# Attention values of the differential heads: one projection of 512 columns in place of two of 256, and a later turn

## Chip, cores and metric

The kernel runs on one core of a Trainium2 chip. The metric is device time in microseconds (us), from the start to the end of one execution.

## What is computed

A macaron layer in fp32 for one sequence of 512 tokens and 1024 features: half a SwiGLU feed-forward, a token mixer, another half feed-forward, each on a normalised input, and a last norm. The change lies in the mixer. Four differential heads (128 wide, two softmax maps each) and eight dilated heads (64 wide) share one input projection. Cut to what matters:

```python
proj = h @ w_in
qa, ka, va, qb, kb, vb = split(proj, each 512 wide)
# differential heads, H=4, two maps of 64 features, values of 128
s = q_blk @ k.T * scale + bias                  # causal, blocks of 128 queries
p = softmax(s);  a = p[:, :, 0] - lam * p[:, :, 1]
oa = rmsnorm(a @ va, subln_gain) * (1 - lam0)
# dilated heads, H=8: three windows, merged by their weights
ob = dilated_attention(qb, kb, vb, ...)
mixed = concat([oa, ob]) @ w_out
```

## The kernel before

Tokens are 4 blocks of 128, features 8 blocks of 128 (KD). Products run on TensorE in fp32r with both operands split into a high and a low part: one product of blocks becomes three (`mm3`: high by high, high by low, low by high). Weights come by DMA in units of 128 x 1024 (512 KB) into a `raw` buffer, of which there are three. ScalarE casts the high part (`high`, line 893), VectorE subtracts for the low part (`low`, line 897), each in two halves of 512 columns; there are three places for split units in `w_all`.

The attention is a schedule written by hand. `plan` lists the stages: q0 to q7 are query and key projections (q0 to q3 of one differential head each, q4 to q7 of two dilated heads each), v0 to v3 the values, 256 features a stage: v0 and v1 of the differential heads, v2 and v3 of the dilated ones. Each stage is 8 chunks of products, and one loop runs over the chunks: iteration t is called step t here. `put(t, rank, f)` hangs other work on a step: ranks below 10 are issued ahead of the step's chunk, others behind it, and within a step by rank. TensorE, VectorE and ScalarE keep the order of issue. At a step's end at most one queued low half and one queued cast are issued; a low half is issued at the earliest one step after its cast. `ahead(n)` at the first use of unit n queues the split of unit n+2 and starts the load of unit n+3.

A query stage takes one step per feature block: three products of 512 columns for queries (`pq`) and three for keys (`pk`). Seven steps after the start its banks are evacuated: `tq` and `tk` (VectorE), casts (ScalarE), rests (VectorE), DMAs to the other half of the partitions; head 0 has a form without DMAs (`evac_now`). A value stage (`v_chunks`) takes two steps for each of 4 token blocks: twelve products a step, with 128 tokens of x as the weights and 256 columns of weights moving, then ScalarE writes the result to a value tile.

`attention(u, s)` hangs a head's own work on the steps from s on: `score` (two products, one VectorE operation that adds the bias and finds the extreme, line 1061, and one exponential on ScalarE, line 1064), one a step; `combine` (lines 1068 to 1075), which merges the two maps of a block. Scores use two PSUM banks in turn. Then, for a differential head, `turn(m, i)`, which transposes the blocks 0..i of query block i by TensorE into a bank with tag `t` (two of them) and copies it by ScalarE, and `values(m, i)`, which multiplies by the values, two steps later. They start at step max(s + 5, end of the head's value stage), in four rounds two steps apart; nine steps after that begin `squares`, `mean`, `scale`, `finish`. In the order before, head 0's scores stand beside v0 and head 1's beside v1.

Product banks (`mm_bank`) have one tag with four buffers, shared by queries, keys, values and each head's output `po`. The tile with tag `tx` (128 x 3072, one buffer) serves the feed-forward and, in the attention, the turned blocks of the dilated heads.

## Time and profile before

| | |
|---|---|
| median of 3 runs | 930.6 us (930.59 to 932.77) |
| profiled execution | 930.6 us, span 928.8 us |
| TensorE (PE) busy | 921.3 us, 99% |
| VectorE (DVE) busy | 727.5 us, 78% |
| ScalarE (ACT) busy | 542.8 us, 58% |
| the attention's steps | about 346 to 545 us |
| value products (`pv`, 3 lines x 128) | 36.3, 36.2 and 36.2 us of records |

Records of products overlap, as a product is issued while the one before it drains; the interval between their starts is what they cost. "Idle before" and the releaser in brackets tell what an engine waited for.

### The profile page before, as it was taken

The page shows a single profiled execution, that of the slowest core. Times are in us where ns is not written, and L with a number is a line of the kernel's source. Part 1 is how long each engine was busy: PE and PEld are TensorE (multiplying, and loading weights), DVE is VectorE, ACT ScalarE, POOL GpSimd, SP SyncE. Part 2 cuts the span into 40 slices and gives each one's busy share as a digit, 9 for nine tenths or more (in the row PEclk, how much of TensorE's full clock was granted, in tenths as well). Part 3 has the DMA queues.
Part 4 walks back from the last instruction along what each step waited for, and adds up shares of the span by engine and source line. Part 5 has one row for each costly group of instructions (what it writes and reads, how often), then busy time and mean ns, then how long its engine had stood idle before and what let it go on. Part 6 is the DMA issues. An engine that isn't in the chain of part 4 may idle for free.

```text
span 928.8 us, 17112 instructions
## 1 busy us (share of the span) xinstructions
PE 921.3 (99%) x6402; PEld 853.8 (92%) x6402; DVE 727.5 (78%) x1501; ACT 542.8 (58%) x1122; POOL 98.3 (11%) x117
## 2 busy tenths in 40 slices
PE   9999999999999999999999999999999999999997
PEld 7889999999999999988979778889999999999997
DVE  7797887677888897668876556797888777888784
ACT  7455664355664575556766664455666455665573
POOL 0001101112202100000000003110111012110100
PEclk9999999999999999999999999999999999999999
DMA  7456646578757562434343113454774677875542
GB/s 259 127 147 149 160 126 178 134 183 223 189 134 201 141 177 92 136 96 129 96 136 92 68 49 132 115 172 103 180 193 118 163 200 191 201 192 149 140 128 91
DMA packets 59860, 136.71 MB, mean 147 GB/s; under 512 B 6832, under 2 KB 8112, under 8 KB 59776
## 3 DMA queue, kind: packets, MB, share of 16 engines
q1 hardware_dynamic: 45776, 110.14, 36.7%
q0 software_dynamic: 14000, 25.47, 17.6%
q8 instruction: 50, 0.82, 0.4%
q14 instruction: 34, 0.28, 0.1%
HBM read 130.30 MB, written 2.14 MB: 143 GB/s over the span
## 4 chain that ended last, share of the span: by engine, by line
PE 97%; DVE 2%; DMA 0%; issue 0%; DVEq 0%
PE pv L935 2%; PE pv L934 2%; PE pv L933 2%; PE pq L123 2%; PE pwo L123 2%; PE pq L124 2%; PE pq L125 2%; PE pk L125 2%; PE pk L123 2%; PE pk L124 2%; PE pwo L124 2%; PE pwo L125 2%; PE pua L123 2%; PE pua L124 2%; PE pua L125 2%; PE pda L124 1%
## 5 line engine op out<-in xcount | busy, mean ns | idle before, releaser
L1064 ACT ACTIVATE pr<-pr,mx 128x128 f32<-128x128 f32 (+3 forms) x64 | 36.0, 563 | 34.4 <-DVE mx L1061 34.1
L1061 DVE CUSTOM_DVE_ANT_0 pr<-sc,strip 128x128 f32<-128x128 f32 (+3 forms) x64 | 30.7, 487 | 22.4 <-PE sc L1059 22.0
L391 ACT CAST w<-s2b 128x512 fp32r<-128x512 f32 x50 | 31.0, 620 | 16.4 <-DVE s2b L373 14.9
L395 DVE TENSOR_TENSOR w<-s2b,w 128x512 fp32r<-128x512 f32 x50 | 34.2, 685 | 7.3 <-ACT w L391 7.3
L391 ACT CAST w<-s2a 128x512 fp32r<-128x512 f32 x46 | 28.6, 621 | 18.7 <-DVE s2a L373 15.8
L395 DVE TENSOR_TENSOR w<-s2a,w 128x512 fp32r<-128x512 f32 x46 | 31.5, 685 | 6.5 <-ACT w L391 6.5
L150 POOL TENSOR_TENSOR sq<-sq,sqt 128x512 f32<-128x512 f32 x7 | 10.9, 1563 | 240.2 <-ACT sqt L149 240.1
L933 PE MATMUL pv<-w,xh 128*128 128x256 f32 x128 | 36.3, 283 | 0.0
L935 PE MATMUL pv<-w,xh 128*128 128x256 f32 x128 | 36.2, 283 | 0.0
L934 PE MATMUL pv<-w,xl 128*128 128x256 f32 x128 | 36.2, 283 | 0.0
L123 PE MATMUL pq<-xh,w 128*128 128x512 f32 x64 | 26.3, 410 | 0.0
L123 PE MATMUL pwo<-mh,w 128*128 128x512 f32 x64 | 25.6, 399 | 0.0
L124 PE MATMUL pq<-xl,w 128*128 128x512 f32 x64 | 25.1, 393 | 0.0
L125 PE MATMUL pq<-xh,w 128*128 128x512 f32 x64 | 25.1, 392 | 0.0
L125 PE MATMUL pk<-xh,w 128*128 128x512 f32 x64 | 25.1, 392 | 0.0
L124 PE MATMUL pk<-xl,w 128*128 128x512 f32 x64 | 25.0, 391 | 0.0
L123 PE MATMUL pk<-xh,w 128*128 128x512 f32 x64 | 25.0, 391 | 0.0
L124 PE MATMUL pwo<-ml,w 128*128 128x512 f32 x64 | 25.0, 390 | 0.0
L125 PE MATMUL pwo<-mh,w 128*128 128x512 f32 x64 | 25.0, 390 | 0.0
L934 PEld LDWEIGHTS pv<-w,xl 128*128 128x128 f32 x128 | 24.5, 191 | 0.3
L933 PEld LDWEIGHTS pv<-w,xh 128*128 128x128 f32 x128 | 24.4, 191 | 0.2
L935 PEld LDWEIGHTS pv<-w,xh 128*128 128x128 f32 x128 | 24.5, 191 | 0.0
(709 smaller groups left out, 3996.9 us busy)
## 6 DMA issues: line engine op xcount, KB each, us to landing
raw_qk<-wqk_dram SPq DMA_DIRECT2D x16, 512.0 KB, 3.4
raw0bg<-wst_dram SPq DMA_DIRECT2D x9, 512.0 KB, 5.1
raw_gua<-wgu_dram SPq DMA_DIRECT2D x8, 512.0 KB, 3.6
raw0ag<-wst_dram SPq DMA_DIRECT2D x8, 512.0 KB, 4.8
raw0ad<-wdg_dram SPq DMA_DIRECT2D x8, 512.0 KB, 5.1
strip<-bias_rows SPq DMA_DIRECT2D x16, 256.0 KB, 3.8
raw_v<-wv_dram SPq DMA_DIRECT2D x8, 512.0 KB, 3.4
raw_wo<-wo_dram SPq DMA_DIRECT2D x8, 512.0 KB, 3.2
```

What stands on the lines that cost most here:

```text
L123: T.matmul(po, wh, mh, start=first, stop=False, skip_group_check=on)
L124: T.matmul(po, wh, ml, start=False, stop=False, skip_group_check=on)
L125: T.matmul(po, wl, mh, start=False, stop=last, skip_group_check=on)
L150: G.tensor_tensor(sq[:], sq[:], t[:], op=ALU.add)
L391: A.copy(made[t][0], source(t))
L395: V.tensor_tensor(l, source(t), h.bitcast(F32), op=ALU.subtract)
L933: T.matmul(po, xh[k][:, xs], wh[:, o:o + 256], start=k == 0, stop=False)
L934: T.matmul(po, xl[k][:, xs], wh[:, o:o + 256], start=False, stop=False)
L935: T.matmul(po, xh[k][:, xs], wl[:, o:o + 256], start=False, stop=k == KD - 1)
L1061: V.tensor_tensor_reduce(out=pi, in0=ps[:, :w], in1=st["b"][m][:, w - 1::-1], op0=ALU.add, op1=ALU.min, scale=1.0, scalar=3.0e38, accum_ou ...
L1064: A.activation(pi, pi, AF.Exp, scale=-1.0, bias=st["mx"][:, m, i:i + 1], accum_out=st["ls"][:, m, i:i + 1])
```

## The change

The stages v0 and v1 become one stage "w" of 16 steps, which stands behind q0 and q1 (steps 16 to 31); the order of the other stages and the number of steps stay. In it each token block takes four steps, one for each weight unit (two feature blocks by 512 columns), with six products of 512 columns. All four units are used for every token block, so all stay in place for the whole stage: three in `w_all`, the third in order in the tile `tx`. The splits and loads around the stage are hung on steps by hand. Head 1's queries, scores and combines move eight steps ahead. The differential heads turn their blocks in three banks (0 and 2, 1, 3) at two steps into `tx`, and multiply all blocks in one step; for heads 0 and 1 this is at steps 32 to 39, behind the stage "w", for heads 2 and 3 at 13 steps behind their first score. The steps of `squares` and after stay for heads 2 and 3.

```diff
-    plan = ["q0", "v0", "q1", "v1", "q2", "q3", "q4", "v2", "q5", "q6", "v3", "q7"]
-    v_end = [8 * plan.index(f"v{u // 2}") + 8 for u in range(8)]
+    plan = ["q0", "q1", "w", "q2", "q3", "q4", "v2", "q5", "q6", "v3", "q7"]
+    start = {w: 8 * i + 8 * (i > 2) for i, w in enumerate(plan)}
+    v_end = [start["w"] + 16] * 4 + [start[f"v{u // 2}"] + 8 for u in range(4, 8)]
...
+            src, nm, own = units[n]
+            if own:
+                raw = wp.tile([P, 1024], F32, tag="raw", name=f"raw_{nm}")
+                nc.sync.dma_start(raw[:], src)
+                more = tp.tile([P, 12 * HS], F32R, tag="tx", name=f"w_{nm}", bufs=1)
+                loaded[n] = raw, more[:, :1024], more[:, 1024:2048]
...
+    def wide_chunks():
+        us = [unit(wvw[c], f"vw{c}", c == 2) for c in range(4)]
+        st, t0 = {}, start["w"]
+        put(t0 - 3, 0, load, us[3])
+        put(t0 - 2, 0, prep, us[2])
+        put(t0, 0, prep, us[3])
+        for i in range(3):
+            put(t0 + 4 + 4 * i, 0, load, us[3] + 1 + i)
+        put(t0 + 13, 0, prep, us[3] + 1)
+        put(t0 + 15, 0, prep, us[3] + 2)
+
+        def chunk(i, c):
+            if c == 0:
+                st["ps"] = mm_bank(f"pvw{i}")
+            po = st["ps"][:]
+            wh, wl = ready[us[c]]
+            xs = slice(i * P, (i + 1) * P)
+            for k in range(2 * c, 2 * c + 2):
+                o = slice(k % 2 * S, (k % 2 + 1) * S)
+                T.matmul(po, xh[k][:, xs], wh[:, o], start=k == 0, stop=False)
+                T.matmul(po, xl[k][:, xs], wh[:, o], start=False, stop=False)
+                T.matmul(po, xh[k][:, xs], wl[:, o], start=False, stop=k == KD - 1)
+            if c == 3:
+                vt[0, i] = slot(i, f"v0{i}")
+                A.activation(vt[0, i][:], po, AF.Copy, scale=held["col"][:, i:i + 1])
+        return [lambda i=i, c=c: chunk(i, c) for i in range(NQ) for c in range(4)]
...
-        def turn(m, i):
-        def values(m, i):
...
+        def turn(tiles):
+            if "tx" not in st:
+                st["tx"] = tp.tile([P, 12 * HS], F32, tag="tx", name=f"ptx{u}", bufs=1)
+            for own in tiles:
+                pt = pp.tile([P, S], F32, tag="t", name=f"pt{u}{own[0]}", bufs=2)
+                n, c0 = 0, st.get("used", 0)
+                for i in own:
+                    st["place", i] = c0 + n
+                    for k in range(i + 1):
+                        o = OFF[i] + k * P
+                        T.transpose(pt[:, n:n + P], st["pr"][0][:, o:o + P], ident[:])
+                        n += P
+                A.copy(st["tx"][:, c0:c0 + n], pt[:, :n])
+                st["used"] = c0 + n
...
-            tv = max(s + 5, v_end[u])
-            for i in range(NQ):
-                put(tv + 2 * i, 2, turn, 0, i)
-                put(tv + 2 * i + 2, 1, values, 0, i)
-            e = tv + 9
+            step, tv = (2, s + 13) if u > 1 else (1, v_end[u] + 3 + 4 * u)
+            put(tv - 2 - step, 2, turn, ((0, 2), (1,)))
+            put(tv - 2, 2, turn, ((3,),))
+            put(tv, 1, values)
+            e = tv + 1
```

`values` now multiplies all four query blocks of a head from `tx`, ten products in one go. On the host the weights are laid out accordingly (`wvw`, four units; `wv` keeps the dilated heads' part).

More of the change, by code (lines that the diff above doesn't have):

```diff
@@ L63, in tile_macaron @@
 @with_exitstack
-def tile_macaron(ctx: ExitStack, tc, xs, xT, wf, wgu1, wst1, wd1, wdg1, wqk, wv, wo, wgu2, wst2, wd2,
+def tile_macaron(ctx: ExitStack, tc, xs, xT, wf, wgu1, wst1, wd1, wdg1, wqk, wvw, wv, wo, wgu2, wst2, wd2,
                  wdg2, lams, relb, onehot, addc, out):
@@ L878, in tile_macaron, with unit @@
     held = {}
-    def unit(src, nm):
-        units.append((src, nm))
+    def unit(src, nm, own=False):
+        units.append((src, nm, own))
         return len(units) - 1
@@ L887, in load @@
         if n < len(units) and n not in loaded:
-            loaded[n] = load_w(*units[n])
+            src, nm, own = units[n]
[4 more added lines that the diff above has]
+                loaded[n] = raw, more[:, :1024], more[:, 1024:2048]
+            else:
+                loaded[n] = load_w(src, nm)
             ready[n] = loaded[n][1:]
@@ L918, in v_chunks @@
         vi, hf = qr // 2, qr % 2
-        us = [unit(wv[qr, c], f"v{qr}{c}") for c in range(2)]
+        us = [unit(wv[hf, c], f"v{qr}{c}") for c in range(2)]
         st = {}
@@ L1023, in evac_now @@
             A.copy(lx[b, :], lx[a, :].bitcast(F32))
-        e = 8 * plan.index(f"q{u}") + 7
+        e = start[f"q{u}"] + 7
         if u in DIRECT:
@@ L1121, in values_part, with values @@
                 n += w
-        def turn(m, i):
-            w = (i + 1) * P
-            pt = pp.tile([P, S], F32, tag="t", name=f"pt{u}{m}{i}", bufs=2)
-            for k in range(i + 1):
-                T.transpose(pt[:, k * P:(k + 1) * P],
-                            st["pr"][m][:, OFF[i] + k * P:OFF[i] + (k + 1) * P], ident[:])
-            ptb = tp.tile([P, S], F32, tag="ptb", name=f"ptb{u}{m}{i}", bufs=2)
-            A.copy(ptb[:, :w], pt[:, :w])
-            st["ptb", m, i] = ptb
-        def values(m, i):
-            if "po" not in st:
-                st["po"] = mm_bank(f"po{u}")
-                st["po3"] = st["po"][:].rearrange("p (i d) -> p i d", i=NQ)
-            fo = (u % 4) * P
-            for k in range(i + 1):
-                T.matmul(st["po3"][:, i, :], st["ptb", m, i][:, k * P:(k + 1) * P],
-                         vt[0, k][:, fo:fo + P], start=k == 0, stop=k == i)
+        def turn(tiles):
[12 more added lines that the diff above has]
+                st["used"] = c0 + n
+        def values():
+            st["po"] = mm_bank(f"po{u}")
+            st["po3"] = st["po"][:].rearrange("p (i d) -> p i d", i=NQ)
+            fo = (u % 4) * P
+            for i in range(NQ):
+                for k in range(i + 1):
+                    o = st["place", i] + k * P
+                    T.matmul(st["po3"][:, i, :], st["tx"][:, o:o + P],
+                             vt[0, k][:, fo:fo + P], start=k == 0, stop=k == i)
         def squares():
@@ L1229, in tile_macaron @@
     for w in plan:
+        if w == "w":
+            chunks += wide_chunks()
+            continue
         chunks += (qk_chunks if w[0] == "q" else v_chunks)(int(w[1]))
@@ L1463, in tile_macaron @@
         {(0, 4): means, (1, 0): spread}, tile_ended, last=last)
-_INS = ["xs", "xT", "wf", "wgu1", "wst1", "wd1", "wdg1", "wqk", "wv", "wo", "wgu2", "wst2", "wd2", "wdg2",
+_INS = ["xs", "xT", "wf", "wgu1", "wst1", "wd1", "wdg1", "wqk", "wvw", "wv", "wo", "wgu2", "wst2", "wd2", "wdg2",
         "lams", "relb", "onehot", "addc"]
@@ L1523 @@
     wqk = pair_tiles(np.concatenate([qa, qb], 1), np.concatenate([ka, kb], 1))
-    wv = np.ascontiguousarray(np.stack([va, vb]).reshape(2, 2, 4, P, 2, 256)
-                              .transpose(0, 4, 1, 3, 2, 5)).reshape(4, 2, P, 1024)
+    wvw = np.ascontiguousarray(va.reshape(4, 2, P, 512).transpose(0, 2, 1, 3)).reshape(4, P, 1024)
+    wv = np.ascontiguousarray(vb.reshape(2, 4, P, 2, 256)
+                              .transpose(3, 0, 2, 1, 4)).reshape(2, 2, P, 1024)
     gcol = lambda g: a(g).reshape(KD, P).T
@@ L1542 @@
         "wqk": wqk,
+        "wvw": wvw,
         "wv": wv,
```

## The prediction

> **What bounds the kernel now.** I read the page first, then the timeline of each engine for the stretch that the change touches. The page gives the span, the busy shares and the chain that ended last:

> ```profile
> span 928.8 us, 17112 instructions
> PE 921.3 (99%) x6402; PEld 853.8 (92%) x6402; DVE 727.5 (78%) x1501; ACT 542.8 (58%) x1122; POOL 98.3 (11%) x117
> PE 97%; DVE 2%; DMA 0%; issue 0%; DVEq 0%
> ```

> TensorE (PE) is busy or queued all the time, and 97% of the chain is PE. The kernel's time is therefore the sum of PE's issue intervals, plus whatever PE has to wait for. The profiled execution took 930.6 us, 1.8 above its span, and the median of the runs is also 930.6, so sums can be made against it directly.

> A busy record is no price for a product here, since records overlap. PE's timeline, with first start, length and product, shows the interval between starts:

> ```profile
> 358.74 0.28 PE L933 MATMUL pv<-w,xh 128*128 128x256 f32 x1
> ...
> 363.77 0.28 PE L933 MATMUL pv<-w,xh 128*128 128x256 f32 x1
> ...
> 366.77 0.28 PE L933 MATMUL pv<-w,xh 128*128 128x256 f32 x1
> ...
> 378.22 0.40 PE L123 MATMUL pk<-xh,w 128*128 128x512 f32 x1
> 379.59 0.39 PE L123 MATMUL pk<-xh,w 128*128 128x512 f32 x1
> ...
> 414.03 0.83 PE L1139 MATMUL po<-v,ptb 128*128 128x128 f32 x6
> 414.69 0.60 PE L1127 MATMUL pt<-ident,pr 128*128 128x128 f32 x4
> 415.05 0.48 PE L123 MATMUL pq<-xh,w 128*128 128x512 f32 x1
> ```

> From 363.77 to 366.77 there are 25 products of 256 columns: 0.120 us each. From 378.22 to 379.59 there are six of 512 columns: 0.228 each (not the 0.39 of their records). The first row is where step 8 of the attention's schedule begins, right behind head 0's query product. Steps 0 to 7 are the same in both kernels.

> What has slack beside PE is seen in the busy time by windows (PE, weight loads, VectorE (DVE), ScalarE (ACT)). The first row is the stretch of values beside head 0's scores, the second one of query products only, with scores, an evacuation of queries and weight splits at once:

> ```profile
> 362.00:374.00 12.00, 12.00 (x93) 11.60 (x92) 7.04 (x26) 9.11 (x24) 0.00 (x0) 1.00 0.14 44
> 422.00:434.00 12.00, 12.00 (x61) 10.12 (x60) 10.63 (x37) 7.63 (x21) 0.00 (x0) 1.00 0.42 125
> ```

> DVE has 5 of 12 us free in the first, hardly more than one in the second. The change makes the first stretch like the second.

> **What the products give.** Removed are v0 and v1: 192 products of 256 columns, 192 x 0.120 = 23.04 us of PE. Added are 96 of 512 columns: 96 x 0.228 = 21.92. The term is **-1.1 us**. That the spacing of two narrow ones is so near to that of a wide one says that only a small fixed part per product is saved (2 x 0.120 - 0.228 = 0.012). [...]

> Without cost on PE: a differential head still issues 10 transposes and 10 value products, in three groups instead of five. A group costs no switch that the intervals show (414.03 to 415.05 is six value records and four transposes, 0.10 each, and the query product is right behind). ScalarE copies a head's turned blocks in three pieces instead of four and evacuates four wide value banks instead of eight narrow ones: less work, on an engine with 3 us free in 12. The weights are four loads of 512 KB as before:

> ```profile
> raw_qk<-wqk_dram SPq DMA_DIRECT2D x16, 512.0 KB, 3.4
> ```

> The fourth one's load moves ahead of head 1's score strips on SP, to step 13, and waits there for a raw buffer, free when unit 4 is split, at 366.8 on the clock below. It lands 3.4 us later, 370.2, 5 us ahead of its cast at 375.2; what is queued behind it on SP is wanted from step 21 on. The third piece lies in the tile tx from step 13 to step 30, and head 0's first turn needs tx at step 32. The bank of the first transposes of step 32 is wanted again one step and 0.66 us later, behind one copy; I put that at zero, at most 0.2.

> **What the denser stretch costs.** Query head 1 now stands at steps 8 to 15, directly behind head 0, and the wide product at 16 to 31 goes through all four weight pieces in its first four steps. So pieces 2 to 4 (units 5, 6, 7) are all split into high (ACT) and low (DVE) parts at steps 12 to 18, one half a step, beside head 0's eight scores, three combines and head 1's evacuation. Unit 7's low halves are queued at steps 17 and 18 and read in step 19. Before, a unit was split eight steps ahead of its use. Whether DVE is there in time is the whole question. This is how DVE spaces such work where it has no rest, in the timeline of before (starts, lengths; scores and evacuation of later heads, low halves):

> ```profile
> 428.00 0.68 DVE L970 SCALAR_TENSOR_TENSOR tq<-pq,rbc_n 128x512 f32<-128x512 f32 x1
> ...
> 429.20 0.16 DVE L1068 RECIPROCAL rl<-ls 128x2 f32<-128x2 f32 x1
> ...
> 429.91 0.42 DVE L1061 CUSTOM_DVE_ANT_0 pr<-sc,strip 128x256 f32<-128x256 f32 x1
> 430.25 1.40 DVE L1001 TENSOR_TENSOR l<-tk,k 64x512 fp32r<-64x512 f32 x2
> 431.69 0.56 DVE L1061 CUSTOM_DVE_ANT_0 pr<-sc,strip 128x384 f32<-128x384 f32 x1
> 432.28 1.39 DVE L1008 TENSOR_TENSOR q<-tq,q 64x512 fp32r<-64x512 f32 x2
> 433.68 0.69 DVE L897 TENSOR_TENSOR w<-raw_v,w 128x512 fp32r<-128x512 f32 x1
> 434.29 0.16 DVE L1068 RECIPROCAL rl<-ls 128x2 f32<-128x2 f32 x1
> ...
> 435.14 0.55 DVE L1061 CUSTOM_DVE_ANT_0 pr<-sc,strip 128x384 f32<-128x384 f32 x1
> ...
> 436.88 0.68 DVE L1061 CUSTOM_DVE_ANT_0 pr<-sc,strip 128x512 f32<-128x512 f32 x1
> 437.49 0.08 DVE L1061 DVE_READ_ACCUMULATOR2_ANT mx<- 128x1 f32 x1
> ```

> Read from start to start: a score 0.34, 0.48 (the 0.55 of its record less the overlap) or 0.61 by its 256, 384 or 512 columns; tq and tk 0.60 each (1.20 from 428.00 to 429.20); the pair l 1.44; a score of 384 ahead of the pair q 0.59; the pair q 1.40; a low half 0.61 (0.60 ahead of a score); a combine 0.71 for block 0 (429.20 to 429.91) and 0.85 for block 1 (434.29 to 435.14). Most start about 0.08 before the one ahead has ended.

> The anchors, and the two waits that the new order makes:

> ```profile
> 364.85 0.62 ACT L893 CAST w<-raw_qk 128x512 fp32r<-128x512 f32 x1
> 365.50 0.69 DVE L897 TENSOR_TENSOR w<-raw_qk,w 128x512 fp32r<-128x512 f32 x1 [1.33 <-ACT w L893]
> 367.00 0.28 DVE L1061 CUSTOM_DVE_ANT_0 pr<-sc,strip 128x128 f32<-128x128 f32 x1
> 367.32 0.40 ACT L1064 ACTIVATE pr<-pr,mx 128x128 f32<-128x128 f32 x1 [0.59 <-DVE mx L1061]
> 413.55 0.69 DVE L970 SCALAR_TENSOR_TENSOR tq<-pq,rbc_n 128x512 f32<-128x512 f32 x1 [1.01 <-PE pq L125]
> 435.76 0.50 PE L1058 MATMUL sc<-k,q 128*128 128x512 f32 x1
> L1064 ACT ACTIVATE pr<-pr,mx 128x384 f32<-128x384 f32 x16 | 9.8, 616 | 10.6 <-DVE mx L1061 10.6
> ```

> PE's side without waits: a step's chunk is 6 x 0.228 = 1.37, a score's two products 0.24, 0.35 (estimate, midway between the two widths) or 0.46. From 358.74, steps 12 to 20 begin at 364.22, 365.83, 367.44, 369.05, 370.66, 372.38, 374.10, 375.93 and 377.76.

> DVE's side, in its queue's order. The first low half of unit 4 stands at 365.50 as before, the second at 366.10, scores 0 and 1 (0.20 each, an estimate: the record's 0.28 less the overlap) behind it at 366.70 and 366.90. The low half queued at step 13 waits for its cast on ACT, which stands behind score 0's exponential: 366.70 + 0.28 + 0.40 + 0.62, with three hand-overs of 0.03 (364.85 + 0.62 to 365.50), 368.09 at the latest; I take 368.08. From there DVE is never free: low 368.08, score 368.68, low 369.10 (0.08 for one of the tiny bounds in between, an estimate, as behind scores 3 to 6), combine 369.70, score 370.41, tq 370.83, tk 371.43, low (unit 6) 372.03, score 372.63, pair l 373.19, low (unit 6) 374.63, combine 375.24, score 5 376.09 to 376.64, pair q 376.76, low (unit 7) 378.16 to 378.85, score 378.76, low (unit 7) 379.45 to 380.14.

> What PE meets: units 5 and 6 are split before steps 17 and 18 read them. At step 19 the score's bank is still being read by score 5. PE follows such a release by 0.07 (435.14 + 0.55 to 435.76), so at 376.71: a wait of 0.78. The chunk's third product, due at 377.63, needs unit 7's first low half, 378.92: a wait of 1.29. The sixth, due at 379.60, needs the second, 380.21: 0.61. Together **+2.7 us**. ACT is not late for any of these: behind tk (372.11) it has four casts of 0.62, the exponential of 0.62 and then unit 7's first cast, 372.11 + 6 x 0.62 = 375.8; the second stands behind score 5's exponential, 376.64 + 2 x 0.62 = 377.9. From step 20 DVE has only scores and combines and catches up within three steps.

> A second wait comes at step 40, where all four product banks are held: both heads' values, pq2 and pk2. pq3 must take pq2's bank. In the row, tq ends at 414.24, 0.21 after the step began at 414.03; with 0.07 for the hand-over this is **+0.3 us**. Before, a fourth bank was free there.

> The sum: -1.1 + 2.7 + 0.3 = +1.9, 930.6 + 1.9 = **932.5 us**. The waits have ends: none at all (929.5) and, with every VectorE operation at its full length, 3.7 us (933.5).

> **Rivals.** *DVE keeps up*: the lag is built of thirteen operations in a row, and if ACT reaches the step-13 cast earlier or low halves come sooner, PE waits for nothing: 930.6 - 1.1 = 929.5. Against it: the windows' 10.63 of 12. *Slower*: the three waits end when the last low half of unit 7 ends; every us that this is later is one us of time. If its operations each start only when the one before has ended, as the pairs l and q do, thirteen of them add 0.08 each, 1.0 us: 933.5. It decides from an end at 381.1 on (380.14 + 0.95), which makes +2.8. [...] *Much faster*: a wide product costs no more than a narrow one when each has its own weight load (loads are busy 11.60 of 12 us in the value stretch): 96 x 0.120 = 11.5 us less, with the waits 922. The query products of the same width speak against it, 0.228. [...]

> **How the numbers follow.** A measurement of this kernel tells about 0.3% (2.8 us) from no change. The forecast with its own range, 931.3 to 933.4, has 0.50, DVE keeping up 0.16, both within 0.3%. Slower, by the lag above or an unforeseen wait of the same kind, 0.30; much faster 0.02 and anything else that is faster 0.02. The range 929.5 to 934.8 reaches from the first rival over the second one with 1 us to spare.

> **What would show it.** Right: the wide products 0.228 apart; before the score and at the third and sixth product of step 19 (the first pass over the fourth weight piece) PE waits for DVE, 2 to 3 us in sum; DVE without a gap from step 13 to 19; 0.3 at head 3's first query product. Wrong: no wait there (929.5), other waits in steps 20 to 40, or a later wait at the values of heads 0 and 1.

## The result, and the profile after

The changed kernel takes 935.23 us (median of 5 runs, 935.05 to 936.70) where the kernel before takes 930.80: 1.0047 of it, 95% interval 1.0036 to 1.0059. It is 4.4 us slower. The forecast was 932.5 with a range up to 934.8.

The page of the kernel after, with the lines that answer to those of before:

```profile
span 933.6 us, 16913 instructions
PE 921.8 (99%) x6306; PEld 848.3 (91%) x6306; DVE 727.2 (78%) x1501; ACT 540.8 (58%) x1114; POOL 98.2 (11%) x117
PE 94%; DVE 4%; issue 1%; ACT 0%; DMA 0%; DVEq 0%; SPq 0%
```

The span grew by 4.8 us, PE has 96 products fewer, and VectorE's share of the chain has doubled: PE now waits. The waits of PE in the attention (who waited for whom: us in total, times, longest), kernel after; before, this view was empty:

```profile
PE pvw L976 <- DVE w L906: 1.4, 2, 1.1
PE ot L1212 <- DVE ob L1206: 1.2, 1, 1.2
PE sc L1095 <- DVE mx L1098: 1.1, 2, 0.6
```

The view counts from the modelled end of the last product, so it shows less than was lost (1.4 for the two waits of `pvw`, which come 1.22 and 0.52 late). The timeline gives the loss in issue intervals. These are PE's products behind a wait, kernel after (start, length, line, tiles, idle and releaser):

```profile
376.94 0.50 PE L1095 MATMUL sc<-k,q 128*128 128x512 f32 x1 [0.60 <-DVE mx L1098]
377.27 0.39 PE L1096 MATMUL sc<-l,q 128*128 128x512 f32 x1
...
379.18 0.50 PE L976 MATMUL pvw<-w,xh 128*128 128x512 f32 x1 [1.05 <-DVE w L906]
...
380.51 0.50 PE L976 MATMUL pvw<-w,xh 128*128 128x512 f32 x1 [0.36 <-DVE w L906]
...
417.36 0.39 PE L125 MATMUL pk<-xh,w 128*128 128x512 f32 x1
417.85 0.50 PE L123 MATMUL pq<-xh,w 128*128 128x512 f32 x1
...
428.23 0.41 PE L1212 MATMUL ot<-ident,ob 128*128 128x128 f32 x2 [1.16 <-DVE ob L1206]
439.53 0.50 PE L1095 MATMUL sc<-k,q 128*128 128x512 f32 x1 [0.54 <-DVE mx L1098]
```

Interval less price (a product of 512 columns 0.228), they come 0.76, 1.22 and 0.52 late at step 19, 0.26 at step 40 (417.36 to 417.85 less 0.23), 1.32 at step 46 and 0.69 at step 52. VectorE's operations that released them, kernel after:

```profile
376.32 0.55 DVE L1098 CUSTOM_DVE_ANT_0 pr<-sc,strip 128x384 f32<-128x384 f32 x1
...
378.44 0.68 DVE L906 TENSOR_TENSOR w<-raw_vw,w 128x512 fp32r<-128x512 f32 x1
...
379.78 0.68 DVE L906 TENSOR_TENSOR w<-raw_vw,w 128x512 fp32r<-128x512 f32 x1
...
417.10 0.69 DVE L1007 SCALAR_TENSOR_TENSOR tq<-pq,rbc_n 128x512 f32<-128x512 f32 x1 [1.62 <-PE pq L125]
...
427.40 0.69 DVE L1206 TENSOR_TENSOR ob<-po,f 128x512 f32<-128x512 f32 x1
...
438.92 0.55 DVE L1098 CUSTOM_DVE_ANT_0 pr<-sc,strip 128x384 f32<-128x384 f32 x1
```

Each ends within 0.15 us of the product that it releases (376.87 and 376.94, 379.12 and 379.18, 380.46 and 380.51, 417.79 and 417.85, 428.09 and 428.23, 439.47 and 439.53). The row at 377.27 shows one more cost, a restart: the first product behind a wait takes 0.33 to the next start instead of 0.228, so each of the five waits ahead of a 512-column product costs 0.1 more.

The account from head 0's first query product to the first output product: 180.30 us before, 184.30 after, +4.0. It is -1.1 (wide products) + 2.50 + 0.26 + 1.32 + 0.55 (0.69 less the 0.14 that the kernel before lost at step 52) + 0.4 (five restarts, where the kernel before has one, behind its wait at step 52), that is 3.9. The rest of the span's difference lies outside: the first product starts 0.27 later, behind the first load, and the stretch behind the attention is 0.5 longer, all of it behind PE's last product.

That the wide products cost what was said is seen in the intervals of the stage w, kernel after:

```profile
385.71 0.40 PE L974 MATMUL pvw<-w,xh 128*128 128x512 f32 x1
385.95 0.40 PE L975 MATMUL pvw<-w,xl 128*128 128x512 f32 x1
386.18 0.39 PE L976 MATMUL pvw<-w,xh 128*128 128x512 f32 x1
386.41 0.40 PE L974 MATMUL pvw<-w,xh 128*128 128x512 f32 x1
386.64 0.39 PE L975 MATMUL pvw<-w,xl 128*128 128x512 f32 x1
386.88 0.39 PE L976 MATMUL pvw<-w,xh 128*128 128x512 f32 x1
387.10 0.28 PE L1095 MATMUL sc<-k,q 128*128 128x256 f32 x1
```

Six take 387.10 - 385.71 = 1.39 us, 0.232 each; the median of all 96 intervals of the stage is 0.228.

### The profile page after: what moved, and what is told of

It reads as the page before. It is cut to its first block, busy times and chain, and to the rows that moved or that the text cites. A ratio compares the mean times of both kernels' runs of the same rounds, so it can differ in the third digit from the quotient of the medians.

```text
span 933.6 us, 16913 instructions
## 1 busy us (share of the span) xinstructions
PE 921.8 (99%) x6306; PEld 848.3 (91%) x6306; DVE 727.2 (78%) x1501; ACT 540.8 (58%) x1114; POOL 98.2 (11%) x117
## 4 chain that ended last, share of the span: by engine, by line
PE 94%; DVE 4%; issue 1%; ACT 0%; DMA 0%; DVEq 0%; SPq 0%
PE pwo L123 2%; PE pwo L124 2%; PE pwo L125 2%; PE pua L124 2%; PE pua L125 2%; PE pua L123 2%; PE pq L123 1%; PE pq L124 1%; PE pq L125 1%; PE pk L123 1%; PE pk L124 1%; PE pk L125 1%; PE pda L125 1%; PE pda L124 1%; PE pub L125 1%; PE pub L123 1%
## 5 line engine op out<-in xcount | busy, mean ns | idle before, releaser
L123 PE MATMUL pq<-xh,w 128*128 128x512 f32 x64 | 26.6, 415 | 0.1
L123 PE MATMUL pwo<-mh,w 128*128 128x512 f32 x64 | 25.5, 399 | 0.0
L123 PE MATMUL pk<-xh,w 128*128 128x512 f32 x64 | 25.1, 392 | 0.0
L125 PE MATMUL pq<-xh,w 128*128 128x512 f32 x64 | 25.0, 391 | 0.0
L125 PE MATMUL pk<-xh,w 128*128 128x512 f32 x64 | 25.0, 391 | 0.0
L125 PE MATMUL pwo<-mh,w 128*128 128x512 f32 x64 | 24.9, 390 | 0.0
L1095 PE MATMUL sc<-k,q 128*128 128x256 f32 (+2 forms) x64 | 21.8, 342 | 1.1 <-DVE mx L1098 1.1
L906 DVE TENSOR_TENSOR w<-raw_qk,w 128x512 fp32r<-128x512 f32 x28 | 18.9, 688 | 3.8 <-ACT w L902 3.7
L1096 PE MATMUL sc<-l,q 128*128 128x256 f32 (+2 forms) x64 | 20.6, 324 | 0.0
L124 PE MATMUL pwgb<-xl,w 128*128 128x256 f32 x72 | 20.2, 281 | 0.0
L125 PE MATMUL pwgb<-xh,w 128*128 128x256 f32 x72 | 20.2, 281 | 0.0
L124 PE MATMUL pxgb<-ttb,w 128*128 128x256 f32 x72 | 20.2, 281 | 0.0
## 6 DMA issues: line engine op xcount, KB each, us to landing
raw_qk<-wqk_dram SPq DMA_DIRECT2D x16, 512.0 KB, 3.4
raw0bg<-wst_dram SPq DMA_DIRECT2D x9, 512.0 KB, 4.6
raw_gua<-wgu_dram SPq DMA_DIRECT2D x8, 512.0 KB, 3.5
raw0ag<-wst_dram SPq DMA_DIRECT2D x8, 512.0 KB, 5.3
raw0ad<-wdg_dram SPq DMA_DIRECT2D x8, 512.0 KB, 4.5
raw_wo<-wo_dram SPq DMA_DIRECT2D x8, 512.0 KB, 3.3
raw_gub<-wgu_dram SPq DMA_DIRECT2D x8, 512.0 KB, 3.2
```

Of the source, the lines that this page charges most:

```text
L123: T.matmul(po, wh, mh, start=first, stop=False, skip_group_check=on)
L124: T.matmul(po, wh, ml, start=False, stop=False, skip_group_check=on)
L125: T.matmul(po, wl, mh, start=False, stop=last, skip_group_check=on)
L906: V.tensor_tensor(l[:, c:c + 512], raw[:, c:c + 512], h[:, c:c + 512].bitcast(F32), op=ALU.subtract)
L1095: T.matmul(ps[:, :n], qs[:, qi], ks[:, :n], start=True, stop=False)
L1096: T.matmul(ps[:, :n], qs[:, qi], ls[:, :n], start=False, stop=True)
```

## The experiments

All start from the changed kernel: most have one edit, three have several, and the last has none. They were timed in five rounds beside the kernel before, which took 931.0 to 931.3 us in these rounds and 930.8 in the result, so the ratio to it, printed with its interval, is to be read against 1.0047 rather than the time against 935.23. (The ratio is taken over all executions and can differ by 0.0003 from that of the two medians.) As the differences are near 1 us, the trace of each says more than its median. "Attention" is again the time from head 0's first query product to the first output product, 184.30 in the kernel after.

**Head 1's last transposes later.** The theory: VectorE's queue is late in each place, for a reason of its own. The rival: it is one lag, and what is taken away in one place is waited for in the next.

```diff
-            put(e + 6, 3, finish)
-            put(e + 7, 8, finish_low)
+            put(e + 6 + 3 * (u == 1), 3, finish)
+            put(e + 7 + 3 * (u == 1), 8, finish_low)
```

> The changed kernel with head 1's last transposes (finish) and the low part behind them three steps later, at steps 49 and 50. Theory (the transposes of step 46 wait 1.3 us because VectorE's queue has not reached head 1's scale): this wait goes, the time falls by about 1.3 us to 933.9 (changed kernel 935.2), and the 2.5 us of waits at step 19 stay. Rival (VectorE's lag is only met one place later, at the scores of steps 47 to 52): the time stays at 935.2 and the score waits there grow by what the transposes no longer wait.

Measured: 934.23 us, 1.0031 (1.0020 to 1.0041). Waits of PE in the attention:

```profile
PE pvw L976 <- DVE w L906: 1.4, 2, 1.0
PE sc L1095 <- DVE mx L1098: 1.0, 2, 0.6
```

The line of `ot` is gone, the others stand as they were (the score of step 52 is 0.61 late, not more). The attention takes 182.92, 1.38 less. The 1.3 us of step 46 are a loss by themselves, and the rival is out here. What VectorE's queue holds there is seen in the kernel after: from 421.33, where the chain of small operations for head 1's scale begins, to 428.09, where the scale ends, it has no gap, and 3.3 us of it are other work (the rests of head 2's queries, two low halves, head 0's low part):

```profile
421.33 0.22 DVE L1199 SCALAR_TENSOR_TENSOR f<-ss,kapt,cs 128x4 f32<-128x4 f32 x1 [0.62 <-ACT ob L1191]
...
421.85 1.41 DVE L1045 TENSOR_TENSOR q<-tq,q 64x512 fp32r<-64x512 f32 x2
423.28 0.69 DVE L906 TENSOR_TENSOR w<-raw_qk,w 128x512 fp32r<-128x512 f32 x1
...
424.76 0.69 DVE L906 TENSOR_TENSOR w<-raw_qk,w 128x512 fp32r<-128x512 f32 x1
425.37 0.75 DVE L1226 SCALAR_TENSOR_TENSOR ml<-ot,sub,mh 128x512 fp32r<-128x512 f32 x1
```

**Head 0's combines later.**

```diff
-            put(s + step * i + (1 if quick else 3 if diff or i < 3 else 2),
+            put(s + step * i + (9 if u == 0 else 1 if quick else 3 if diff or i < 3 else 2),
```

> The changed kernel with head 0's four combines at steps 21, 23, 25 and 27 instead of 15, 17, 19 and 21: 1.56 us of VectorE work fewer ahead of score 5 and of the fourth piece's low halves. Theory (VectorE's full queue is what PE waits for at step 19): score 5 is read 1.56 earlier than 0.76 late, so no wait, the low halves' waits (1.22 and 0.52) end 1.56 earlier: 0.0 to 0.2 us in all are left, time 932.8. Rival (the low halves are late because of their casts on ScalarE): only the score's wait goes, 934.5.

Measured: 933.96 us, 1.0031 (1.0020 to 1.0042). VectorE's low halves of the fourth piece, in this run:

```profile
376.99 0.68 DVE L906 TENSOR_TENSOR w<-raw_vw,w 128x512 fp32r<-128x512 f32 x1
...
378.32 0.68 DVE L906 TENSOR_TENSOR w<-raw_vw,w 128x512 fp32r<-128x512 f32 x1
```

They stand 1.45 and 1.46 us ahead of those in the kernel after (0.10 of it because the attention's first product starts earlier), most of the 1.56 of VectorE work that was taken out, so it is VectorE's queue and not the casts that makes them late. The score's wait is gone. Yet the products behind it still wait 0.70 and 0.54: the expectation took 1.56 off each wait, which is wrong. The three waits of step 19 are one lag met three times; PE that doesn't wait for the score is earlier at the low half. In sum they fell from 2.50 to 1.24, the attention by 1.36. The 932.8 was added up wrongly; the cause stands.

**Head 1's turn and tail two steps later.**

```diff
-            step, tv = (2, s + 13) if u > 1 else (1, v_end[u] + 3 + 4 * u)
+            step, tv = (2, s + 13) if u > 1 else (1, v_end[u] + 3 + 6 * u)
```

> The changed kernel with head 1's turn, values and all that follows two steps later (values at 41 instead of 39). Theory: at step 40 only three product banks are held, so the 0.26 us ahead of head 3's first query product go; head 1's scale is wanted at step 48 and not at 46, so the 1.3 us go as well or shrink to under 0.4: time 933.7 to 934.1. Rival (the lag is only met later): at or above 935.0, with longer score waits at steps 47 to 52.

Measured: 933.85 us, 1.0026 (1.0016 to 1.0036). In the trace the waits of step 40 and of head 1's transposes are both gone, and the score of step 52 is 0.65 late, no more than before the edit. Head 3's first query product starts at 416.35 there, while `tq` still reads query head 2's bank (415.85 to 416.54): it has a bank of its own. So the 0.26 is the product bank that head 1's output held, as forecast. (The attention takes 183.75 in this trace, with about 1.1 of a clock drop in it that the last section describes.)

**The two together.**

```diff
-            put(s + step * i + (1 if quick else 3 if diff or i < 3 else 2),
+            put(s + step * i + (9 if u == 0 else 1 if quick else 3 if diff or i < 3 else 2),
...
-            step, tv = (2, s + 13) if u > 1 else (1, v_end[u] + 3 + 4 * u)
+            step, tv = (2, s + 13) if u > 1 else (1, v_end[u] + 3 + 6 * u)
```

> The changed kernel with head 0's combines at steps 21 to 27 and head 1's turn and tail two steps later, that is the edits of the second and third run together. Theory (each wait is paid for by itself, VectorE's queue being the cause in each place): the savings add, 1.3 and 1.6 us: 932.3. Rival (a lag that is taken away in one place comes back in the next): 933.8, as either alone.

Measured: 932.30 us, 1.0015 (1.0006 to 1.0024). In its trace the attention takes 181.15, 3.15 less than in the kernel after, where the first of the two edits alone took off 1.36 and the second about 1.65 (184.30 less 183.75, and the 1.1 of the clock drop). The savings of lags in separate places add. Three of the eleven executions took 934.3 to 934.7, the profiled one (934.48) among them. In that one the loss lies ahead of the attention, which starts at 348.94 instead of 346.68: the kernel's first products stand 0.43 us apart up to 9.85 us, in the kernel after 0.23 from 5.54 on.

**The weights of the wide stage split earlier.** The second and the fourth unit get slots that the heads 4 to 7 use later, so they need not wait for a place. Of the edit this shows the steps; the slots are left out:

```diff
...
-        put(t0 - 3, 0, load, us[3])
-        put(t0 - 2, 0, prep, us[2])
-        put(t0, 0, prep, us[3])
+        put(t0 - 6, 0, prep, us[1])
+        put(t0 - 6, 0, load, us[2])
+        put(t0 - 5, 0, load, us[3])
+        put(t0 - 4, 0, prep, us[2])
+        put(t0 - 2, 0, prep, us[3])
```

> The changed kernel with only the weights of the wide stage earlier: its second and fourth unit get places of their own, and units 5, 6 and 7 are split from steps 10, 12 and 14 on instead of 12, 14 and 16. Theory: the last low half is done three operations earlier and VectorE's idle 0.8 us before step 13 is used, so both low-half waits (1.22 and 0.52) go; but both halves of unit 7 now stand ahead of score 5, which ends 0.4 later, so the score's wait grows from 0.76 to about 1.2: net -1.3, 933.9. Rival (order does not matter, only the amount of VectorE work up to step 19): -0.8, 934.4.

Measured: 933.84 us, 1.0028 (1.0016 to 1.0039). Waits of PE in the attention:

```profile
PE sc L1112 <- DVE mx L1115: 1.4, 2, 0.8
PE ot L1229 <- DVE ob L1223: 1.2, 1, 1.2
```

Both low-half waits are gone, and the score of step 19 is 0.98 late instead of 0.76. A new small wait (0.27) stands at step 14, where the earlier low halves are ahead of the first scores. That the time comes out as forecast is in part luck: the score's wait was to grow to 1.2, and 0.98 and the unforeseen 0.27 make the same sum. So here the order of VectorE's queue decided what PE waits for, and its amount how much is left (0.98 and 0.27, in sum 1.25, where the three waits of step 19 made 2.50).

**Head 2's first combine later.**

```diff
-            put(s + step * i + (1 if quick else 3 if diff or i < 3 else 2),
+            put(s + step * i + (8 if (u, i) == (2, 0) else 1 if quick else 3 if diff or i < 3 else 2),
...
-            step, tv = (2, s + 13) if u > 1 else (1, v_end[u] + 3 + 4 * u)
+            step, tv = (1 + (u == 3), s + 13) if u > 1 else (1, v_end[u] + 3 + 4 * u)
```

> The changed kernel with head 2's first combine at step 53 instead of 48 and its first turn at 55 instead of 54. Theory (the score of step 52 waits for VectorE, since the transposes that stood ahead of it in the kernel before have moved behind it): 0.71 us of VectorE work less ahead, the wait of 0.69 falls to under 0.1: 934.6. Rival (the combine only moves the wait to the turn): 935.2.

Measured: 935.04 us, 1.0044 (1.0032 to 1.0057), which can't be told from the 1.0047 of the changed kernel. In the trace the score of step 52 is 0.42 late instead of 0.69. Most of the 0.71 taken out did not arrive there, and a row of this run shows where half of it went: VectorE now stands idle for 0.35 us until ScalarE has cast head 3's keys:

```profile
434.62 0.68 DVE L1038 TENSOR_TENSOR l<-tk,k 64x512 fp32r<-64x512 f32 x1 [0.35 <-ACT k L1019]
```

So VectorE's queue releases this score, but about half of what the combine costs there hides behind a wait for ScalarE.

**All of these at once.**

These are the edits of the second, third, fifth and sixth run; the first is left out, as the third moves the same transposes.

> All of these edits at once: early split, head 0's combines later, head 1's tail two steps later, head 2's first combine and turn later. Theory: the four places with waits (steps 19, 40, 46, 52; 2.5, 0.3, 1.3 and 0.7 us) are clear and the 1.1 us of the wide products remain as a gain: 930.0 to 930.5, below the kernel before by 0.3 to 1.1. Rival: waits come up in other places, 932 or more.

Measured: 930.79 us beside 931.22 for the kernel before: 0.9998 (0.9989 to 1.0007), no difference that can be told. The attention takes 179.72, 0.58 less than before the change. Waits of PE in it:

```profile
PE sc L1112 <- DVE mx L1115: 0.2, 1, 0.2
```

By intervals two scores are late, 0.24 at step 14 and 0.36 at step 52; with their restarts that is the half microsecond that is missing to the 1.1 us. So the waits are the whole of the slowdown, and what the wide product itself can bring is no more than the intervals said.

**A further version.** The edit against the run with all edits; head 2's combine and turn, not shown, go back to where they were:

```diff
-        put(t0 - 6, 0, prep, us[1])
+        put(t0 - 5, 0, prep, us[1])
...
-            put(e + 2, 9, rests_q)
+            put(e + 2 + (u == 3), 9, rests_q)
```

> As the run with all edits, but unit 5 is split from step 11 on instead of 10 (the score of step 14 waited 0.24 us there), head 2 has its combine and turn back at 48 and 54, and head 3's query rests stand one step later, behind score 5 of head 2 (the score of step 52 waited 0.36 with the combine moved). Theory: both waits fall below 0.1, the attention from head 0's first query product to the output projection takes 179.2 us (180.30 before, less the 1.1 of the wide products), time 930.2 beside 931.2 for the kernel before. Rival: other waits of VectorE come up, 930.8 or more, no difference from before.

Measured: 931.15 us, 1.0001 (0.9992 to 1.0010); the attention takes 180.02. Both waits are gone, but at step 53 head 3's first score is 0.84 late. The profile names no releaser for it ("issue"). It starts 0.11 us behind the end of VectorE's operation on the score of step 51, whose bank it takes by the order of the two banks, so this is the likely cause:

```profile
436.71 0.68 DVE L1115 CUSTOM_DVE_ANT_0 pr<-sc,strip 128x512 f32<-128x512 f32 x1
437.50 0.36 PE L1112 MATMUL sc<-k,q 128*128 128x256 f32 x1 [0.68 <-issue]
```

Here the rival was right: between steps 47 and 53 the lag was only moved on by one step. No version tried is faster than the kernel before.

**The price of the products by itself.** The changed kernel with each wide product as two of 256 columns:

```diff
-                T.matmul(po, xh[k][:, xs], wh[:, o], start=k == 0, stop=False)
-                T.matmul(po, xl[k][:, xs], wh[:, o], start=False, stop=False)
-                T.matmul(po, xh[k][:, xs], wl[:, o], start=False, stop=k == KD - 1)
+                for m, w, first, last in ((xh, wh, k == 0, False), (xl, wh, False, False),
+                                          (xh, wl, False, k == KD - 1)):
+                    for f in (0, HS):
+                        T.matmul(po[:, f:f + HS], m[k][:, xs], w[:, o.start + f:o.start + f + HS],
+                                 start=first, stop=last, skip_group_check=True)
```

> The changed kernel with every wide product done as two of 256 columns, the order of everything else untouched: 192 products in place of 96. Theory of the price (0.012 us fixed per product): +1.1 us on PE, of which some 0.3 come back because the four steps 16 to 19 are longer and the waits at step 19 shorter: 936.0. Rival (wide products save much more, their loads being hidden): 940 or more.

Measured: 936.38 us, 1.0055 (1.0043 to 1.0068), 1.15 more than the changed kernel. In the trace the attention is 0.77 longer while the score of step 19 waits 0.22 less (0.54). So 96 products more cost 0.99, 0.010 each, near the 0.012 of the forecast.

**The changed kernel once more.**

> The changed kernel once more beside the kernel before and the run with all edits, on one chip: 1.0047 of before as in the first result, with the same six waits at the same steps in its trace; where the clock is granted in full the attention takes 184.3 us.

Measured: 935.78 us, 1.0054 (1.0042 to 1.0067). The six waits stand at the same steps (0.76, 1.22, 0.49, 0.26, 1.32, 0.70). The attention takes 185.44, not 184.30, for the reason in the last section.

## Why the prediction was wrong

- *The products, -1.1 us*: right. The wide ones stand 0.228 apart in the stage w, and made narrow again they cost 0.99 more.
- *Step 19, +2.7 us*: right in place, order and size. Forecast 0.78, 1.29 and 0.61, found 0.76, 1.22 and 0.52, in sum 2.5. The last low half was to end at 380.14 and ended at 380.46 in a trace whose first product starts 0.27 later.
- *Step 40, +0.3 us*: right, 0.26, and it goes when the bank is free.
- *The slower rival by longer VectorE operations*: not what happened. The intervals were those of the rows: in the kernel after 0.60 from the low half at 378.44 to the score at 379.04, 0.61 from there to 379.65. The low half itself started while the operation ahead, 378.31 and 0.21 long, still ran:

```profile
378.31 0.21 DVE L865 TENSOR_SCALAR kape<-kap 128x1 f32<-128x1 f32 x1
378.44 0.68 DVE L906 TENSOR_TENSOR w<-raw_vw,w 128x512 fp32r<-128x512 f32 x1
379.04 0.69 DVE L1098 CUSTOM_DVE_ANT_0 pr<-sc,strip 128x512 f32<-128x512 f32 x1
379.65 0.08 DVE L1098 DVE_READ_ACCUMULATOR2_ANT mx<- 128x1 f32 x1
```

- *The step that failed* is the list of places where PE meets VectorE: it ended at step 40. The prediction put the new turn, three groups instead of five, under "Without cost on PE", by the number of its products, and let VectorE catch up within three steps of step 20. It did not follow what the move does to the meeting of the two engines further on. It left out two such places and one term:
  - *Step 46, 1.32 us.* Head 1's tail (squares, mean, three Newton steps, scale) moved from steps 43 to 47 to steps 40 to 44, beside the rests of head 2's queries and head 0's low part, and its `finish` from step 49 to 46. The run with later transposes takes this wait away alone.
  - *Restarts, 0.4 us.* The sum had no term for them, though the kernel before has one: its score of step 52 starts at 435.76 and the next product at 436.09, 0.33 later.
  - *Step 52, 0.55 us more than before.* In the kernel before, PE had more to do ahead of this score: from the score of step 48 it took 8.05 us to it, 0.14 of them a wait. In that stretch stood four transposes of head 1's `finish` (0.36) and, of head 2's turn and values, three transposes and two products (0.61). In the kernel after all of these are elsewhere, and the stretch takes 7.58 us, 0.70 of them a wait: PE is there 1.03 us sooner, VectorE's operation that frees the bank only 0.46 (it starts 7.43 us behind the score of step 48 before, 6.97 after). The run with later transposes puts head 1's `finish` back at step 49. VectorE's operation then starts 7.33 us behind the score of step 48, almost as late as before, and the score is still 0.61 late, so it is the 0.61 of head 2's turn and values that PE lacks. PE's rows of the kernel before, then the rows of that run:

```profile
427.71 0.28 PE L1058 MATMUL sc<-k,q 128*128 128x256 f32 x1
...
431.50 0.27 PE L1127 MATMUL pt<-ident,pr 128*128 128x128 f32 x1
...
435.18 0.38 PE L1139 MATMUL po<-v,ptb 128*128 128x128 f32 x2
435.39 0.38 PE L1127 MATMUL pt<-ident,pr 128*128 128x128 f32 x2
```

```profile
429.87 0.28 PE L1095 MATMUL sc<-k,q 128*128 128x256 f32 x1
...
437.20 0.55 DVE L1098 CUSTOM_DVE_ANT_0 pr<-sc,strip 128x384 f32<-128x384 f32 x1
...
437.81 0.50 PE L1095 MATMUL sc<-k,q 128*128 128x512 f32 x1 [0.45 <-DVE mx L1098]
```

The three make 2.3 us. By the spans the kernel after is 4.8 longer where the forecast was 1.9; of the 2.9 between them, 0.8 lies outside the attention, and the waits of steps 19 and 40 came 0.2 smaller than forecast.

- *The chances*: the 0.66 for no change rested on the two waits being all. Above the forecast the range had room for 2.3 us (934.8), and the time, 935.23, lies 0.4 beyond it. One of its signs of being wrong, "other waits in steps 20 to 40", ends six steps ahead of the first wait that was missed.

## What to carry to other kernels

Where PE ran without a gap, making products wider gained only the fixed part of each, here 0.010 to 0.012 us from 256 to 512 columns; read it from intervals between starts (0.228), not from the lengths of records (0.39). When a schedule is moved, list every place where the busiest engine takes something from another one, for all that moves and all that stays, to the end of the schedule, and follow the other engine's queue to each. Waits that came from one lag were paid once and could not be summed one by one (1.56 us less VectorE work took 1.26 off the three waits of step 19 together); lags in separate places did add (3.15 with both edits, 1.36 and 1.65 with one each).

## What the runs showed of the hardware

In three traces (head 1's turn and tail later, head 2's combine later, and the changed kernel once more) the clock granted to PE falls to half right behind the waits of step 19. Busy time by windows of the changed kernel once more (PE, weight loads, DVE, ACT, POOL, then the granted clock):

```profile
376.00:379.60 3.60, 1.95 (x7) 1.16 (x7) 3.54 (x10) 1.32 (x4) 0.00 (x0) 1.00 0.61 184
379.60:383.00 3.40, 3.31 (x8) 2.12 (x8) 2.50 (x11) 1.84 (x5) 0.00 (x0) 0.50 0.48 118
383.00:386.40 3.40, 3.40 (x18) 2.85 (x18) 1.48 (x6) 1.35 (x5) 0.00 (x0) 1.00 0.50 190
```

The products in the slow stretch start 0.43 us apart instead of 0.23:

```profile
381.42 0.63 PE L975 MATMUL pvw<-w,xl 128*128 128x512 f32 x1
381.85 0.63 PE L976 MATMUL pvw<-w,xh 128*128 128x512 f32 x1
```

It lasts 3.4 us and costs about 1.1 (185.44 less 184.30). The first profile of the changed kernel has the same waits, PE is also busy for 1.95 of the 3.60 us, and there is no such drop:

```profile
376.00:379.60 3.60, 1.95 (x8) 1.05 (x7) 3.54 (x8) 1.42 (x4) 0.00 (x0) 1.00 0.60 190
379.60:383.00 3.40, 3.04 (x15) 2.20 (x14) 2.51 (x11) 1.73 (x5) 0.00 (x0) 1.00 0.59 92
```

```profile
376.17:379.59 3.42, 1.77 (x7) 1.15 (x7) 3.36 (x10) 1.22 (x3) 0.00 (x0) 1.00 0.60 184
```

```profile
377.23:380.64 3.41, 2.00 (x8) 0.99 (x8) 3.35 (x10) 1.72 (x5) 0.00 (x0) 1.00 0.31 123
```

The first holds the two longest waits whole, and the clock is at half behind it; the second does not, and the clock stays full. The stretches ahead of the fall at the end, of the kernel before and of the kernel after:

```profile
922.06:925.48 3.42, 0.93 (x9) 0.69 (x7) 2.08 (x7) 1.26 (x2) 0.00 (x0) 1.00 0.76 273
```

```profile
926.77:930.19 3.42, 0.49 (x5) 0.25 (x3) 1.77 (x5) 1.26 (x2) 0.00 (x0) 1.00 0.76 276
```

In these two traces PE is busy for 2.00 us or more in every other whole stretch, as this profile models it, and the clock is full behind each. The clock thus fell behind stretches with 0.49, 0.93 and 1.77 us of PE and stayed full behind those with 2.00 or more. That is what these three traces show; no run was made to try it.

In the stretch ahead of the drop PE was not idle but busy for about half of it (1.77 of 3.42 us). With the drop, the waits of step 19, 2.5 us in sum, cost 1.1 more. In the result, one execution of the changed kernel (936.70) has a mean granted clock of 0.997 and the other four (935.05 to 935.36) 0.998, which such a drop would explain (half of 3.41 us is 0.002 of the 934, an estimate); that one was not profiled.
